# One hybrid block in fp32 on one core: two token streams interleaved by weight tiles, a lasting weight pool, and a recut gate table

## The chip, the core and the metric

The kernel runs on one core of a Trainium2 chip. TensorE (PE) multiplies, VectorE (DVE), ScalarE (ACT) and GpSimd (POOL) do element-wise work, SyncE (SP) issues DMAs; each has its own in-order instruction stream, and they meet at semaphores. Operands lie in SBUF, results of matmuls in eight PSUM banks. The metric is the device time of one launch in microseconds (us), a median over runs.

## The reference

512 tokens of width 2048, in float32, go through one block of three layers, each followed by a residual and a layer norm (`x = layer_norm(2^0.25 * x + h)`):

```
# 1: mixer
ml_q, ml_k, ml_v, ml_o, ml_i, ml_f, fx_q, fx_k, fx_v, fx_f, g_ml, g_fx = split(x @ w_in)
ml_q, ml_k = silu(causal_conv4(ml_q, ml_k))
h = norm(mlstm(ml_q, ml_k, ml_v, ml_i, ml_f)) * sigmoid(ml_o)      # 4 heads, 256 / 512 wide
y = forgetting_attention(fx_q, fx_k, fx_v, fx_f)                   # 16 heads of 128
h = (sigmoid(g_ml) * (h @ w_br_ml) + sigmoid(g_fx) * (y @ w_br_fox)) @ w_out
# 2: attention to a memory of 256 rows, 4 heads of 512
h = softmax((x @ w_xq) @ k.T) @ v @ w_xo          # k, v = split(mem @ w_xkv)
# 3: product-key experts: 8 heads, each 16 of 128*128 experts
i, g = top16 of (x @ peer_wq) against two sets of 128 keys per head
h = sum over the 128 chosen of  gelu(x . expert_u[i]) * g * expert_v[i]
```

The kernel makes each large product of three matmuls in fp32r, which carries fewer bits than fp32: an operand is split into `hi` (rounded) and `lo` (the rest), and `hi*hi + hi*lo + lo*hi` is summed in PSUM.

## The kernel before

**Streams.** The 512 tokens make two paths (class `Path`, L303): A is the first block of 128 tokens, B the other 384. A runs ahead, since B's mLSTM and attention read A's keys and values from DRAM scratch. The last layer treats tokens in two ways: for A's 128 and for the last 96 tokens the chosen experts' rows are gathered (`gathered`, L842, by indirect DMA on POOL's queue: 256 and 192 row sets of 128 x 8 KB); for the 288 between (`NDENSE`) all experts are computed densely, with a table of gates that is zero where an expert isn't chosen.

**Weight tiles.** A weight matrix comes in groups of 512 columns, a group as eight tiles of 128 x 1024 floats (512 KB). `load_w` (L160) takes one: SP loads it into a `raw` slot (`load_raw`, L125), ACT casts it to `whi` (L120), DVE subtracts to `wlo` (L123), every eighth POOL instead (L122, `SHARE`). A weight pool sets how many slots of each there are: `w1` has 5 raw, 3 hi and 2 lo and ends with the first block and the heads; `w2` 5, 3, 3 up to the end of B's attention; `w3` 3, 2, 2 after that; and `V` 3, 3, 3 for `expert_v` in the main loop. `group_ws` (L188) holds the weights still and streams 384 or 256 tokens (24 matmuls a tile), `group_as` (L203) holds the tokens still and streams the weights: 6 matmuls a tile for A, 18 for B. Matmuls of both are at L185 (`products`). PSUM has five banks `mm` for groups, and `s1`, `s2` for small products.

**Order.** Each stage is a generator that yields after a whole group. `run` (L915) drives one and, after yields whose numbers are listed by hand, lets another do its next group:

```
run(mlstm(A, ...), memory(mp), [3 * h + i for h in range(ML_H) for i in (1, 2)])
run(chain(branch_ml(A, HA, aq), fox(A, a3, at, hold_y)), heads, (5, 13, 24))
run(merge(A, YA, GA, ac, at), heads, (4,))
run(tail_a(), heads, (4, 7, 9, 13, 14))
```

So A's mLSTM takes turns with the memory's projections (L333), then A's other stages with `heads`, the mLSTM of B (L1002). `mids` (L144) is a list of small steps (softmax, transposes), of which `ride` does one after each weight tile. The framework's scheduler then orders each engine's stream by its own model, within the dependencies.

**In order of time** (us in the profile): x is loaded and split, and the gates' projections and cumulative sums made (to about 45, L236 to L287); A's mLSTM and the memory's projections (to 440); A's branches, attention (`fox`, L497), merge, `w_out` (`residual`, L633), norm (L657), cross-attention (L689), top-k, woven with the heads (to 1500); B's branches and attention (to 2410), during which the jobs of A's gathered rows go on; then the 16 tiles of y are loaded (`ytd`, L1064 to L1069: load into a work tile, split into a pair), and B's merge, `w_out`, norms and cross-attention follow (to 3100).

**The dense experts.** After B's `peer_wq`, top-k runs on DVE while `stage_a` (L1174) already multiplies: for one chunk of 128 experts two tiles of `uT`, 48 matmuls of 288 tokens, gelu, and where the result must wait, a store to DRAM (`gad`, L1188, from ACT's queue). `LOOK` = 64 chunks come before the main loop. Among them the gate table is built (L1132 to L1160): for six parts of 48 tokens, DVE makes one-hot rows (L1146, L1152), PE multiplies them (L1154), ACT copies them to four `stage` tiles (L1157), and four DMAs on ACT's queue store them (L1159):

```
gd = dp.tile([P, NC_ // 2, NDENSE // GB, 2, GB], ...)
nc.scalar.dma_start(gd[:, ch * 16:ch * 16 + 16, hb], stage[ch].rearrange("p (c q) t -> p c q t", q=2))
```

that is, in each partition 16 pieces of 2 x 48 floats. In the main loop, for each eight chunks and each quarter of the output, `stage_o` (L1214) multiplies `expert_v` tiles (24 matmuls each) by `hp`, which `stage_h` (L1192) makes from the gelu and the gate table (loaded for two chunks at a time, L1195, one piece of 2304 B a partition). Sums are added on DVE into `acc` (L1243). `fill` (L1269) puts in the remaining `stage_a` chunks and the gathered jobs of the last 96 tokens, 194 jobs: 20 (`EARLY`) before the loop, the others spread up to chunk 124. `fin` (L898) ends with the last norm and the stores.

## Time and profile before

| | |
|---|---|
| time, median of 3 runs | 5120.34 us (5119.35 to 5123.38) |
| the profiled execution | 5116.37 us, of which the span from the first to the last instruction is 5114.7 us |
| instructions in it | 74819 |
| DMA | 1421.00 MB, 278 GB/s in the mean |
| mean granted clock of PE | 0.98 |

The page of the profile has the busy time of each engine, its course in 40 slices, the DMA queues, the chain of work that ended last, and the costliest groups of instructions. Other views, which the prediction uses, are read so: "windows" gives for a stretch its length, then for each engine the busy us and the number of instructions, then PE's granted clock, the share of the DMA engines that was busy, and GB/s. "Waits" has rows `who <- whom: us in total, times, longest`. "Timeline" has start, duration, engine, line and operation, in brackets the idle time before it and what ended it. A row of "source" has the least, median and largest duration in ns. A group's row ends with busy us and mean ns of one, then idle time before it. A matmul's end is modelled, so the step from one start to the next, not the duration, is its pace.

### The profile page before, as it was taken

To read this page: it belongs to the slowest core of one execution; us is meant where nothing else is said; L and a number is where in the kernel's file an instruction comes from. 1 tells how busy PE (TensorE), PEld (TensorE's weight loads), DVE (VectorE), ACT (ScalarE), POOL (GpSimd) and SP (SyncE) were. 2 spreads that over 40 slices of the span, in tenths; PEclk is the share of its full clock that TensorE was granted. 3 is DMA by queue.
4 is the path that set the end of the run, shared out by engine and by line. 5 is a ranking of instruction groups with operands and counts; after the bars stand their busy time and mean duration, and the time that the engine had idled before them with its cause. 6 is when DMAs were issued, how large, how long until landed. Compare 5 with 4: busy or idle time off the path is not lost. (4 is left out here: it accounts for less than half of the span.)

```text
span 5114.7 us, 74819 instructions
## 1 busy us (share of the span) xinstructions
PE 4801.1 (94%) x28401; PEld 4370.3 (85%) x28401; DVE 3708.1 (72%) x5387; ACT 2114.1 (41%) x3043; POOL 1312.4 (26%) x1039
## 2 busy tenths in 40 slices
PE   7999999999999999998999999999899999999886
PEld 6877777777779999987988879998899999999875
DVE  6666676656788677776876566897667878788786
ACT  5656675455533233332324333344334333434322
POOL 1112223121233444422532312320011212122222
PEclk9999999999999999999999999999999999999998
DMA  6777897666679899876976755566689989898994
GB/s 228 270 268 260 282 312 254 221 228 206 199 280 367 335 337 345 310 266 256 348 295 235 254 204 192 201 221 203 195 309 346 347 316 359 314 356 330 341 346 178
DMA packets 405626, 1421.00 MB, mean 278 GB/s; under 512 B 93004, under 2 KB 129484, under 8 KB 346224
## 3 DMA queue, kind: packets, MB, share of 16 engines
q1 hardware_dynamic: 248032, 827.14, 46.3%
q0 software_dynamic: 89408, 551.06, 28.4%
q10 hardware_dynamic: 67824, 38.02, 2.5%
q8 instruction: 222, 3.64, 0.3%
q14 instruction: 140, 1.15, 0.1%
HBM read 1343.32 MB, written 72.62 MB: 277 GB/s over the span
## 5 line engine op out<-in xcount | busy, mean ns | idle before, releaser
L120 ACT CAST whi<-raw 128x1024 fp32r<-128x1024 f32 x1472 | 1531.6, 1051 | 2137.2 <-PE mm L185 1027.1
L123 DVE TENSOR_TENSOR wlo<-raw,whi 128x1024 fp32r<-128x1024 f32 x1352 | 1687.3, 1261 | 813.3 <-ACT whi L120 398.3
L864 DVE SCALAR_TENSOR_TENSOR xacc<-rows,dots,xacc 128x2048 f32<-128x2048 f32 x224 | 534.2, 2385 | 212.7 <-DMA rows<-in_peer_v,eid 211.7
L837 POOL DMA_INDIRECT rows<-in_peer_v,eid x224 | 356.2, 1590 | 984.0 <-DVE wlo L123 307.4
L837 POOL DMA_INDIRECT rows<-in_peer_u,eid x224 | 327.1, 1460 | 1095.4 <-DVE rows L851 443.1
L185 PE MATMUL pa<-Ch,whi 128*128 128x288 f32 x2048 | 565.0, 300 | 42.3 <-ACT whi L120 40.9
L185 PE MATMUL po<-hph,whi 128*128 128x288 f32 x2048 | 552.3, 298 | 28.6 <-ACT whi L120 14.9
L185 PE MATMUL pa<-Cl,whi 128*128 128x288 f32 x2048 | 561.7, 298 | 0.0
L185 PE MATMUL po<-hpl,whi 128*128 128x288 f32 x2048 | 549.8, 297 | 0.0
L851 DVE SCALAR_TENSOR_TENSOR rows<-rows,xacc 128x2048 f32<-128x2048 f32 x224 | 518.0, 2321 | 43.6 <-DMA rows<-in_peer_u,eid 43.2
L122 POOL TENSOR_TENSOR wlo<-raw,whi 128x1024 fp32r<-128x1024 f32 x120 | 306.5, 2554 | 849.0 <-PE mm L185 428.3
L185 PE MATMUL mm<-xh,whi 128*128 128x384 f32 x1280 | 436.1, 343 | 10.2 <-ACT whi L120 4.2
L185 PE MATMUL mm<-whi,xh 128*128 128x512 f32 x1088 | 431.4, 397 | 11.6 <-ACT whi L120 10.8
L185 PE MATMUL mm<-xl,whi 128*128 128x384 f32 x1280 | 430.1, 337 | 0.0
L185 PEld LDWEIGHTS pa<-Ch,whi 128*128 128x128 f32 x2048 | 390.3, 191 | 46.4 <-ACT whi L120 43.5
L185 PE MATMUL mm<-whi,xl 128*128 128x512 f32 x1088 | 425.7, 391 | 0.0
L185 PEld LDWEIGHTS po<-hph,whi 128*128 128x128 f32 x2048 | 383.9, 190 | 36.9 <-ACT whi L120 17.7
L185 PEld LDWEIGHTS pa<-Cl,whi 128*128 128x128 f32 x2048 | 390.5, 191 | 0.0
L185 PEld LDWEIGHTS po<-hpl,whi 128*128 128x128 f32 x2048 | 384.6, 190 | 0.8 <-issue 0.8
L185 PE MATMUL po<-hph,wlo 128*128 128x288 f32 x2048 | 335.8, 298 | 19.9 <-DVE wlo L123 19.9
L185 PE MATMUL mm<-wlo,xh 128*128 128x512 f32 x1088 | 320.3, 403 | 15.4 <-DVE wlo L123 11.8
L185 PE MATMUL pa<-Ch,wlo 128*128 128x288 f32 x2048 | 326.9, 296 | 4.5 <-DVE wlo L123 4.5
(425 smaller groups left out, 8441.8 us busy)
## 6 DMA issues: line engine op xcount, KB each, us to landing
raw<-in_w_in SPq DMA_DIRECT2D x512, 512.0 KB
raw<-in_vq SPq DMA_DIRECT2D x256, 512.0 KB
raw<-in_uT SPq DMA_DIRECT2D x256, 512.0 KB
raw<-in_w_xkv SPq DMA_DIRECT2D x64, 512.0 KB
raw<-in_w_br_ml SPq DMA_DIRECT2D x64, 512.0 KB
raw<-in_w_br_fx SPq DMA_DIRECT2D x64, 512.0 KB
raw<-in_w_out SPq DMA_DIRECT2D x64, 512.0 KB
raw<-in_w_xq SPq DMA_DIRECT2D x64, 512.0 KB
```

The lines of the kernel that those rows point to most:

```text
L120: nc.scalar.copy(hi, src)
L122: return nc.gpsimd.tensor_sub(lo, src, hi.bitcast(F32))
L123: return nc.vector.tensor_sub(lo, src, hi.bitcast(F32))
L185: nc.tensor.matmul(o, w if stat else x, x if stat else w, start=k == first and x is xh and not part, stop=k == last and part == 1)
L837: i = nc.gpsimd.indirect_dma_start(out=rows, out_offset=None, in_=I[table], in_offset=bass.IndirectOffsetOnAxis(ap=ei[:, k:k + 1], axis=0))
L851: nc.vector.scalar_tensor_tensor(rows, rows, 1.0, xacc, op0=ALU.mult, op1=ALU.mult, accum_out=dots[:, k:k + 1])
L864: nc.vector.scalar_tensor_tensor(xacc, rows, dots[:, k:k + 1], xacc, op0=ALU.mult, op1=ALU.add)
```

## The change

First, all groups yield after each weight tile, and a new `weave` drives two generators by a rate:

```diff
                 products(todo, 0, 15)
                 ride()
+                if kt < 7:
+                    yield
             for t in range(nt):
                 evac(t, banks[t])
+            yield 1 if nt == 1 else None
...
+        def weave(gen, other, rate):
+            due = 0.0
+            for extra in gen:
+                due += rate if extra is None else extra
+                while due >= 1:
+                    due -= 1
+                    next(other, None)
...
+                first = mlstm(A, a1, dict(ka=1, pre=2, qk=6, v=2, o=2, nM=1, pt=2), hold_h)
+                for _ in range(8):
+                    next(first)
...
+                gts.close()
+                with tc.tile_pool(name="mem", bufs=1, reuse_waits="tile") as mp:
+                    mem = memory(mp)
+                    weave(first, mem, 52 / 77)
+                    run(mem)
...
+                weave(chain(branch_ml(A, HA, aq), fox(A, a3, at, hold_y)), heads, 0.045)
+                weave(iter([2]), heads, 0)
                 settle()
+            weave(chain(merge(A, YA, GA, ac, at), tail_a()), heads, 0.045)
```

In place of the "..." after the eight `next` stand the transposes of the gates, which came ahead of the first group. So A's tile brings 0.045 tiles of the heads, the end of an A group a whole one, and four and two more stand ahead of and behind each norm in `tail_a` (`yield 4`, `yield 2`). A's groups and norms take their PSUM bank from a pool of their own, `ma`, with one bank, until B is alone (then five `mm` again); the two numbers are those of `mm` and `ma`:

```diff
+        banks(bk, "ps1", 4, 1)
...
-            banks = [mm_bank() for _ in range(nt)]
+            banks = [mm_bank() if nt > 1 else ma_bank() for _ in range(nt)]
```

Second, one weight pool `W` lasts for the whole kernel, and a list of rings is gone through in turn, one ring a load. The three numbers are the raw, hi and lo slots; `xs` closes after B's attention, `E` is opened ahead of the top-k, both serve from the first `stage_a` on, and `V` is gone:

```diff
+        W = weights(ctx, "w", 3, 2, 2)
+        rings[:] = [W, weights(xs, "w1", 2, 1, 1), W]
...
+        def load_raw(src, n=1024):
+            rings.append(rings.pop(0))
+            ring = rings[-1]
...
         xs.close()
+        rings[:] = [W]
-        weights(ctx, "w3", 3, 2, 2)
...
+        E = weights(ctx, "w2", 3, 3, 3)
...
+        rings[:] = [W, E]
```

Third, h and y are loaded straight into the lo tile of their pair, and y lazily, five ahead of its use in the merge, over the memory that x held (the x pools now free tile by tile):

```diff
+        def load_split(hi, lo, src):
+            nc.sync.dma_start(lo.bitcast(F32), src)
+            nc.scalar.copy(hi, lo.bitcast(F32))
+            nc.vector.tensor_sub(lo, lo.bitcast(F32), hi.bitcast(F32))
...
-            YB = []
-            for j in range(16):
-                y = tmp()
-                nc.sync.dma_start(y, ytd[j])
-                YB.append(pair(apool, "A", [P, B.n], 32))
-                split(*YB[j], y)
+                    while len(self) < min(16, j + 5):
+                        self.append(pair(apool, "A", [P, B.n], 32))
+                        load_split(*list.__getitem__(self, -1), ytd[len(self) - 1])
```

Fourth, the gate table is stored in pieces of 32 x 48 floats and loaded for four chunks at a time, and the dense stage's numbers move:

```diff
-        gd = dp.tile([P, NC_ // 2, NDENSE // GB, 2, GB], F32, tag="gd", name="gd")
+        gd = dp.tile([P, NDENSE // GB, NC_, GB], F32, tag="gd", name="gd")
...
-                nc.scalar.dma_start(gd[:, ch * 16:ch * 16 + 16, hb],
-                                    stage[ch].rearrange("p (c q) t -> p c q t", q=2))
+                nc.scalar.dma_start(gd[:, hb, ch * 32:ch * 32 + 32], stage[ch])
...
-        LOOK = 64
-        EARLY = 20
+        LOOK = 68
+        EARLY = 44
...
-            if c % 2 == 0:
-                gt = mn.tile([P, NDENSE // GB, 2, GB], F32, tag="G", bufs=2, name=nm("G"))
-                nc.sync.dma_start(gt, gd[:, c // 2])
+            if c % 4 == 0:
+                gt = mn.tile([P, NDENSE // GB, 4, GB], F32, tag="G", bufs=2, name=nm("G"))
+                nc.sync.dma_start(gt, gd[:, :, c:c + 4])
...
-            a, b = pair(mn, "hp", [P, NDENSE], 2 * J + 4)
+            a, b = pair(mn, "hp", [P, NDENSE], 2 * J + 2)
...
-                    while turn_g[0] < njobs - EARLY and turn_g[0] * (NC_ - 4) <= c * (njobs - EARLY):
+                    while turn_g[0] < njobs - EARLY and turn_g[0] * (NC_ - 16) <= c * (njobs - EARLY):
```

The last line spreads the gathered jobs up to chunk 112 instead of 124. Some work tiles have other numbers of slots (`aq` 11 for 10, `at` 5 for 6, `ht` 1 for 2, `rst` 1 for 2).

255 lines of the change are left out of this document (126 added, 129 removed).

## The prediction

> **What bounds the kernel now.** First the page: which engine is nearly always busy.
>
> ```profile
> PE 4801.1 (94%) x28401; PEld 4370.3 (85%) x28401; DVE 3708.1 (72%) x5387; ACT 2114.1 (41%) x3043; POOL 1312.4 (26%) x1039
> ```
>
> TensorE (PE) is the bound; the change takes no matmul away (both programs hold the same number), so it can only win PE's stops: 5114.7 - 4801.1 = 314 us of visible idle, and what the modelled matmul ends hide. Second, busy time by stretch; columns are PE, weight load, DVE, ACT, POOL, then granted clock, DMA share and GB/s.
>
> ```profile
> 0.00:70.00 70.00, 39.42 (x220) 31.36 (x221) 51.24 (x107) 43.87 (x77) 13.92 (x25) 0.83 0.66 223
> 70.00:440.00 370.00, 356.38 (x1865) 293.72 (x1864) 242.12 (x343) 222.42 (x269) 74.42 (x62) 1.00 0.80 268
> 440.00:1500.00 1060.00, 1006.78 (x4552) 793.10 (x4551) 717.18 (x1210) 578.40 (x791) 251.67 (x231) 0.99 0.71 244
> 1500.00:1560.00 60.00, 51.62 (x288) 50.55 (x287) 50.96 (x68) 20.28 (x29) 23.80 (x18) 0.94 0.93 351
> 2410.00:2440.00 30.00, 14.53 (x69) 13.26 (x70) 15.66 (x20) 10.54 (x19) 7.90 (x12) 0.77 0.93 336
> 3100.00:3480.00 380.00, 369.29 (x2597) 365.89 (x2596) 310.68 (x868) 149.95 (x212) 92.73 (x66) 1.00 0.58 194
> 3480.00:3750.00 270.00, 226.89 (x1664) 222.33 (x1663) 181.33 (x386) 104.53 (x328) 7.82 (x7) 0.92 0.70 208
> 3750.00:4780.00 1030.00, 1024.80 (x7713) 1020.20 (x7712) 808.33 (x896) 399.47 (x507) 219.15 (x143) 1.00 0.90 337
> 4780.00:5115.00 335.00, 249.37 (x1705) 234.57 (x1703) 263.13 (x325) 91.66 (x112) 74.96 (x49) 0.91 0.75 281
> ```
>
> Idle PE, stretch less busy: start 30.6; first block's mLSTM beside the memory projections 13.6; first block beside the heads 53.2; second weight pool 8.4; Y loaded 15.5; top-k 10.7; gate table 43.1; main loop 5.2; tail 85.6. The clock adds to it: 0.92 over 270 us is, at a half speed, 2 x 0.08 x 270 = 43 us throttled, 22 us lost. The sum below is made against the profiled execution, 5116.37 us (span 5114.7 and 1.7 around it), 4.0 us under the median of 5120.34.
>
> **Part by part. 1. Weaving by weight tiles.** Two paces of PE, from starts of matmuls that follow each other:
>
> ```profile
> 504.45 0.39 PE L185 MATMUL mm<-whi,Ch 128*128 128x512 f32 x1
> 504.69 0.39 PE L185 MATMUL mm<-whi,Cl 128*128 128x512 f32 x1
> ```
>
> ```profile
> 467.23 0.33 PE L185 MATMUL mm<-xh,whi 128*128 128x384 f32 x1
> ...
> 470.00 1.55 PE L185 MATMUL mm<-xh,wlo 128*128 128x384 f32 x8
> 471.38 0.33 PE L185 MATMUL mm<-xh,whi 128*128 128x384 f32 x1
> ```
>
> A tile of the first block is six matmuls, 6 x 0.235 = 1.41 us; one of the other stream is 471.38 - 467.23 = 4.15 us. Each is 524,288 bytes, so a run of the first block's tiles asks 372 GB/s; no stretch above moves more than 351. What a run does reach, in the queue's timeline:
>
> ```profile
> 500.74 19.10 SPq L128 DMA_DIRECT2D raw<-in_w_br_ml  x11
> ```
>
> and who waits from 440 to 1480 us (total, times, longest):
>
> ```profile
> SPq L128 <- DVE wlo L123: 560.3, 279, 11.1
> ACT whi L120 <- DMA raw<-in_w_in: 47.2, 73, 3.4
> PE mm L185 <- DVE wlo L123: 23.1, 40, 1.9
> PE mm L185 <- ACT whi L120: 13.2, 20, 2.1
> ```
>
> Eleven issues in 19.10 us are ten steps of 1.88 us. The queue waits for raw slots, casts wait for landings, PE for the split: supply is short in such runs, while an 8-tile group of the other stream (33 us) leaves the queue idle with its five slots full. Woven, eight first-block tiles bring 7 x 0.045 + 1 = 1.3 tiles of the heads: 8 x 1.41 + 1.3 x 4.15 = 16.7 us for 9.3 tiles, 292 GB/s, under what the rows show. The gain lies between the visible 53 us and 40 groups x 8 x (1.88 - 1.41) = 150; nothing is the lower end if DVE's bursts, not supply, make the stops. I take **75**: half the upper end, since norms and softmax chains keep theirs. For the stretch before, 13.6 us idle, I take 8 of 0 to 14. The Trainium skill, page "DMA: Bandwidth & Descriptors", section Specifications, puts a core's HBM limit at about 358 GB/s. By it the run of 372 must stop and the woven 292 need not, which would give 95 here and 4910 us in all; the 351 of 1500 to 1560 agrees with such a ceiling.
>
> The price: first-block groups now share one PSUM bank ("ma"), so the next group's first matmul waits for the copy that empties it.
>
> ```profile
> L120 ACT CAST whi<-raw 128x1024 fp32r<-128x1024 f32 x1472 | 1531.6, 1051 | 2137.2 <-PE mm L185 1027.1
> ```
>
> ```profile
> L320 ACT COPY at<-mm x36: 573/586/599, 39.1 to 1371.6; 128x512 f32<-128x512 f32 x36
> ```
>
> The copy is 0.59 us, with a cast of 1.05 ahead of it on ACT at most 1.64; 56 groups, 0 to 92 us. In the new instruction order a tile of the other stream, up to 4.15 us, stands between most groups and covers it: **-10**. The tiles' splits are the same instructions; lo has three slots where it had two, hi three and raw five as before.
>
> **2. Start.** The gate transposes stand behind ten tiles instead of eight, but ahead of the first memory tile, so PE still waits for the gate chain: two tiles' 2.8 us, I take 3 of the 30.6.
>
> **3. One lasting pool.** At 1500 to 1560 the second pool no longer waits for the first one's buffers: 5 of the idle 8.4, bounds 0 and 8. In top-k (idle 10.7) uT tiles have six raw and five hi and lo slots instead of three and two; DVE, 310.68 of 380 busy, is the other limit: 5, bounds 0 and 11.
>
> **4. Y over x.** At 2410 one wait stands out:
>
> ```profile
> PE mm L185 <- ACT Ah L120: 15.2, 1, 15.2
> ```
>
> Sixteen loads and splits stood between attention and merge; now each row lands in its lo tile, five ahead, and the merge's matmuls follow the attention's directly. The first row must still wait for x's last reader and for DMA, cast and split. 15.2 idle and half of the throttled 2 x 0.23 x 30 = 14 make 22; I take **15**, bounds 5 and 22.
>
> **5. Gate table in large pieces.** Issue times in ns (least, median, most) of its stores on ACT's queue, of ACT's store of 128 pieces of 1152 B (gad) and of SP's load of 128 pieces of 4096 B (uT); then ACT's timeline around three gate stores; then that stretch's waits:
>
> ```profile
> L1159 ACTq DMA_DIRECT2D gd<-stage x24: 377/2607/6355, 3489.4 to 3730.4; - x24
> ...
> L1188 ACTq DMA_DIRECT2D gad<-ga x126: 326/327/2018, 3243.9 to 4777.8; - x126
> ```
>
> ```profile
> L128 SPq DMA_DIRECT2D raw<-in_uT x256: 327/328/877, 3204.5 to 4754.2; - x128
> ```
>
> ```profile
> 3625.95 11.55 ACTq L1159 DMA_DIRECT2D gd<-stage x3
> 3637.61 1.99 ACT L120 CAST whi<-raw 128x1024 fp32r<-128x1024 f32 x2 [11.60 <-issue]
> ```
>
> ```profile
> ACT whi L120 <- issue: 56.2, 7, 12.3
> PE pa L185 <- ACT whi L120: 34.2, 7, 8.4
> ```
>
> Three issues hold ACT for 11.55 us, casts stand behind them, and PE stands for the casts: 34.2 us, and 22 us of clock, 56 together. The new store has 128 pieces of 6144 B instead of 2048 of 384 B; by the gad and uT rows, alike over a factor of 3.6 in bytes, 24 issues cost 8 us instead of 24 x 2.6 = 63. DVE is late next: the new order has 19 gathered rows beside these matmuls where this stretch had 8,
>
> ```profile
> L851 DVE SCALAR_TENSOR_TENSOR rows<-rows,xacc 128x2048 f32<-128x2048 f32 x8 | 18.3, 2292 | 10.8 <-DMA rows<-in_peer_u,eid 10.8
> ```
>
> so 181 + 11 x 2.3 = 207 of about 215 us. Hence **40**, not 56; bounds 15 and 56. The Trainium skill, same page, section "Issuing engines are not separate DMA queues", says that the sequencer's time to initiate a DMA is usually small beside the DMA. By it this term would be nearly nothing and the time 4970, as in rival C. The rows differ: 11.55 us of issue for three stores, with the casts behind it. The loads of G go the other way, 768 pieces instead of 128, 32 instead of 64 of them: on SP, whose waits are for slots, and in a loop where PE idles 5 us in 1030: I take 2 lost with the two "hp" slots fewer, bounds 0 and 10.
>
> **6. Gathers done earlier.** From 4780 on a wait, the pace of the main loop's matmuls, and PE's last stretch on the chain:
>
> ```profile
> DVE xacc L864 <- DMA rows<-in_peer_v,eid: 23.9, 12, 6.9
> ```
>
> ```profile
> 3799.88 0.29 PE L185 MATMUL po<-hph,whi 128*128 128x288 f32 x1
> 3800.01 0.30 PE L185 MATMUL po<-hpl,whi 128*128 128x288 f32 x1
> ```
>
> ```profile
> 5075.30 1.26 PE po L1249 x10
> ```
>
> DVE stands for gathered rows, with splits and PSUM adds queued behind. The stretch's 1705 matmuls at 0.132 us are 225 us; with the 38 us from 5076.6 to the end 263, against 335: 72 us lost. In the new order the last gathered row stands 35 DVE splits of 3.2 us ahead of the end (before: two), and rows come singly, not in threes; 44 of the 194 jobs move to the quieter stretch before. The 38 us of output stay: **50**, bounds 20 and 72.
>
> Sum: 75 + 8 - 10 + 3 + 5 + 5 + 15 + 40 - 2 + 50 = 189. 5116.4 - 189 = 4927, and with 4 to the median **4930**.
>
> **Rivals.** *A: weaving yields nothing*, because DVE's bursts (conversions, softmax, one tensor after another) and not supply stop PE: DVE is 717 of 1060 busy there, and PE's two rows name the split more than the cast. Then 75 and 8 go, 106 is left: 5116 - 106 + 4 = 5014. *B: slower, by POOL's splits.* Every eighth tile is split on POOL:
>
> ```profile
> L122 POOL TENSOR_TENSOR wlo<-raw,whi 128x1024 fp32r<-128x1024 f32 x120 | 306.5, 2554 | 849.0 <-PE mm L185 428.3
> ```
>
> Before, that tile was always the last of its group, and another stream's loads often came next; woven, it falls anywhere, and with one lo slot in the small pool and a fixed rotation all loads behind it stand. The 64 memory, 448 first-block and 72 heads' tiles up to 1500 us hold 584 / 8 = 73 of them; if each shows its 2.55 us, 186 are lost against 189 - 83 = 106 won elsewhere: 5116 + 80 + 4 = 5200. It decides from 106 / 73 = 1.5 us a tile. Against it: a heads' tile of 4.15 us is longer than POOL's split. *C: the gate term is nothing*, because a store of 768 KB holds ACT however it is cut, or DVE takes PE's place as what is late: 40 goes, 4970; the uT row, 0.33 us for 512 KB, speaks against the first. *D: the change doesn't do what it says*, the scheduler undoing the weave: the new instruction order shows 24 matmuls of the heads inside nearly every first-block group, so I leave it out.
>
> **Chances.** Forecast, 4860 to 4985 with C in it: 0.62. A, 4985 to 5060: 0.20. B and other losses of its size: 0.10, of which a tenth lands near no change. Better than 4860, where weaving, tail and gate reach their upper ends (94 more in all): 0.08. The range **4860 to 5040** holds 0.8. About 0.2% (10 us) is what a measurement here can tell from no change: faster 0.88, same 0.03, slower 0.09.
>
> **What would show it.** Right: the queue's loads of first-block tiles evenly 1.8 us apart and PE idle of 440 to 1500 halved; the gate stores under 0.5 us each and no cast waiting for issue; no wait for "Ah"; no gathered row in the last 100 us, PE busy to its last matmul. Wrong: PE waiting for POOL's split or for the "ma" copy (B), PE idle before 1500 unchanged (A), or the main loop no longer at 1024.8 of 1030 because the woven slots or the shorter "hp" ring starve it.

## The result, and the profile after

| | before | after |
|---|---|---|
| median of 4 runs | 5121.86 us (5119.35 to 5124.33) | 5068.13 us (5062.06 to 5072.05) |
| the profiled execution | 5116.37 us, span 5114.7 | 5072.05 us, span 5070.3 |
| after / before | | 0.9894, 95% interval 0.9877 to 0.9911 |

The changed kernel is 54 us faster. 4930 was forecast, so 138 us of the forecast gain are missing. The page of the changed kernel, busy time of each engine:

```profile
PE 4789.3 (94%) x28401; PEld 4397.2 (87%) x28401; DVE 3728.7 (74%) x5387; ACT 2122.9 (42%) x3046; POOL 1270.4 (25%) x1039
```

Visible idle time of PE is 5070.3 - 4789.3 = 281 us instead of 314. Its stretches, cut where the stages end in this kernel (length, busy time of PE, weight load, DVE, ACT, POOL, granted clock, DMA share, GB/s):

```profile
0.00:70.00 70.00, 41.47 (x209) 32.30 (x210) 54.09 (x109) 42.04 (x76) 12.92 (x25) 0.80 0.69 233
70.00:430.00 360.00, 349.04 (x1884) 297.79 (x1883) 247.08 (x332) 216.96 (x265) 75.45 (x58) 1.00 0.81 269
430.00:1425.00 995.00, 961.47 (x4456) 784.87 (x4456) 724.91 (x1203) 573.28 (x790) 251.21 (x236) 0.99 0.77 261
1425.00:1555.00 130.00, 112.88 (x590) 105.03 (x589) 92.84 (x127) 41.01 (x59) 43.52 (x31) 0.92 0.83 306
2385.00:2460.00 75.00, 54.41 (x232) 48.77 (x231) 38.06 (x39) 18.46 (x33) 22.13 (x25) 0.85 0.69 240
3460.00:3740.00 280.00, 266.57 (x2025) 263.71 (x2024) 233.58 (x429) 123.57 (x329) 26.09 (x22) 0.98 0.75 272
3740.00:3800.00 60.00, 39.69 (x269) 37.08 (x268) 37.23 (x96) 20.46 (x74) 1.70 (x2) 0.86 0.60 216
3800.00:4900.00 1100.00, 1080.01 (x8017) 1069.23 (x8016) 892.32 (x981) 430.26 (x529) 232.54 (x157) 0.99 0.92 343
4900.00:5040.00 140.00, 127.72 (x908) 121.99 (x909) 78.99 (x117) 44.89 (x54) 4.50 (x5) 0.95 0.45 149
```

The first block's stretch idles 33 us in 995, where it was 53 in 1060; the gate table's stretch 13 in 280, where it was 43 in 270; the last stretch 12 in 140, where it was 86 in 335 (38 of these the output). But 1425 to 1555, the merge at 2385 and the first 60 us of the main loop have new holes, and the main loop stops for 20 us in 1100, where it was 5 in 1030.

**A ledger.** The stages lie at other times in the two kernels, so they are compared at equal work: for every start of a matmul, the usual step (from one start to the next, of matmuls of its shape, 30th percentile in the trace of before) is summed; a run is "ahead" by the time that it reaches the same sum earlier. One run is good to some 5 us either way, so two can differ by 10 for no cause: seven kernels whose code is the changed kernel's up to the end of the first block are 38.8 to 48.6 ahead there. What one stage wins or loses is steadier. Columns: the time at which the kernel before has done that much work, and its stage; last, the difference of the spans. All in us, positive is ahead of the kernel before.

| run | 434 memory | 1474 first block | 2001 B's branches | 2562 y, merge | 3447 top-k | 3698 gate table | 3814 loop starts | 4725 loop | span |
|---|---|---|---|---|---|---|---|---|---|
| after | 9.5 | 48.6 | 42.0 | 9.4 | 2.5 | 28.8 | 16.1 | -14.2 | 44.4 |
| weave8 | -28.2 | -98.7 | -102.0 | -125.6 | -120.6 | -97.0 | -112.1 | -151.6 | -89.6 |
| weave8_mm5 | -0.3 | -43.7 | -51.3 | -62.4 | -60.1 | -36.5 | -49.5 | -84.7 | -21.7 |
| listed | -8.1 | -34.4 | -64.9 | -105.1 | -111.3 | -79.5 | -107.2 | -150.0 | -89.5 |
| before_rings | -3.0 | -31.3 | -49.8 | -57.9 | -64.4 | -61.0 | -60.8 | -63.5 | -55.2 |
| one_ring | 12.2 | 67.9 | 61.6 | 18.7 | 17.7 | 40.4 | 26.5 | -9.9 | 50.6 |
| one_ring_eager | 15.9 | 72.3 | 66.5 | 41.2 | 38.9 | 57.1 | 35.5 | -0.8 | 55.7 |
| eager_y | 9.8 | 41.7 | 35.2 | 16.7 | 14.3 | 41.6 | 28.2 | -5.5 | 56.6 |
| before_gate | 0.7 | -3.1 | -5.9 | -5.5 | -6.9 | 38.2 | 53.1 | 41.8 | 2.6 |
| before_half | -2.1 | -3.1 | -6.2 | -4.8 | -12.2 | -8.2 | -7.6 | -25.9 | 22.8 |
| before_gate_half | -2.3 | -2.3 | -5.4 | -3.6 | -11.5 | 35.8 | 49.5 | 11.2 | 60.3 |
| after_half | 9.1 | 44.7 | 38.2 | 13.4 | 20.7 | 52.6 | 22.0 | -27.8 | 36.9 |
| apart | 8.9 | 41.4 | 34.1 | 2.8 | -2.3 | 23.3 | 37.2 | 14.3 | 24.4 |
| apart_fast | 9.0 | 45.2 | 37.0 | 10.8 | 9.0 | 36.0 | 50.3 | -60.2 | 14.8 |
| late | 6.6 | 38.8 | 32.2 | 3.9 | 2.8 | 41.2 | 30.9 | 3.1 | 37.7 |
| before_turn | 0.3 | -0.3 | -3.8 | -4.5 | -11.1 | -9.6 | -17.7 | -32.0 | 12.1 |
| before_early | 0.2 | 4.6 | 1.8 | 4.6 | -23.6 | -38.4 | -47.9 | -52.3 | -7.3 |
| hybrid_eager | 9.5 | 48.0 | 42.4 | 25.3 | 19.1 | 44.9 | 59.4 | -8.4 | 52.7 |
| best_mid | 14.4 | 71.0 | 65.7 | 47.6 | 45.4 | 69.9 | 54.1 | 23.3 | 79.2 |

The row of the changed kernel says where to look: 49 us won up to the end of the first block, nearly all of them lost again by 3447, 26 won by the gate table and 43 lost in the main loop, 59 won in the last stretch.

### The profile page after: what moved, and what is told of

Its sections match the earlier page's. It is cut to its first block, busy times and chain, and to the rows that moved or that the text cites. A ratio compares the mean times of both kernels' runs of the same rounds, so it can differ in the third digit from the quotient of the medians.

```text
span 5070.3 us, 74427 instructions
## 1 busy us (share of the span) xinstructions
PE 4789.3 (94%) x28401; PEld 4397.2 (87%) x28401; DVE 3728.7 (74%) x5387; ACT 2122.9 (42%) x3046; POOL 1270.4 (25%) x1039
## 5 line engine op out<-in xcount | busy, mean ns | idle before, releaser
L846 POOL DMA_INDIRECT rows<-in_peer_v,eid x224 | 336.0, 1500 | 1010.8 <-DVE wlo L137 389.5
L205 PE MATMUL pa<-Ch,whi 128*128 128x288 f32 x2048 | 564.8, 300 | 14.4 <-ACT ga L1223 13.0
L846 POOL DMA_INDIRECT rows<-in_peer_u,eid x224 | 309.6, 1382 | 1037.1 <-DVE rows L860 320.4
L205 PE MATMUL po<-hph,whi 128*128 128x288 f32 x2048 | 533.6, 298 | 32.6 <-ACT hph L134 27.3
L205 PE MATMUL po<-hpl,whi 128*128 128x288 f32 x2048 | 533.1, 297 | 6.1 <-DVE hpl L137 6.1
L205 PEld LDWEIGHTS pa<-Ch,whi 128*128 128x128 f32 x2048 | 389.8, 190 | 18.3 <-ACT ga L1223 14.8
L205 PE MATMUL po<-hph,wlo 128*128 128x288 f32 x2048 | 349.5, 298 | 6.0 <-DVE wlo L137 6.0
L205 PEld LDWEIGHTS po<-hph,wlo 128*128 128x128 f32 x2048 | 301.5, 191 | 6.5 <-DVE wlo L137 6.5
L205 PEld LDWEIGHTS pa<-Ch,wlo 128*128 128x128 f32 x2048 | 289.8, 189 | 4.7 <-DVE wlo L137 3.9
L205 PE MATMUL mm<-xh,wlo 128*128 128x384 f32 x1280 | 258.5, 337 | 5.3 <-DVE wlo L137 5.3
```

The costliest lines, as they stand in the source:

```text
L205: nc.tensor.matmul(o, w if stat else x, x if stat else w, start=k == first and x is xh and not part, stop=k == last and part == 1)
L846: i = nc.gpsimd.indirect_dma_start(out=rows, out_offset=None, in_=I[table], in_offset=bass.IndirectOffsetOnAxis(ap=ei[:, k:k + 1], axis=0))
```

## The experiments

Each time below is a median; the ratio is to the kernel before on the same chip, with its 95% interval. The runs lie on several chips, so differences of a few us go by the ratios. The changed kernel's is 0.9894, 5068 us.

### The first block: tiles, banks, rings

**weave8.** The other stream driven in whole groups, at the rates of the change.

```diff
-                while due >= 1:
-                    due -= 1
-                    next(other, None)
+                while due >= 8:
+                    due -= 8
+                    for _ in range(8):
+                        next(other, None)
```

> Base is the changed kernel, 5068 us. The same rates, but the other stream is driven eight tiles (a whole group) at a time instead of single tiles; banks and rings as changed. Theory S (the supply of weight tiles is short in runs of the first block, and mixing by tiles evens it out; 50 us were won up to the end of the first block at equal work): 30 to 50 us more, 5098 to 5118. Rival A of the prediction (DVE's bursts stop PE, and what was won there came from elsewhere, such as the sixth lo slot or the bank of its own): 5068 within 6.

5204.59 us, 1.0163 (1.0145 to 1.0182): 136 us more than the changed kernel, far above the 30 to 50 expected. Who waits in it from 440 to 1480 us:

```profile
PE ma L205 <- ACT at L340: 43.4, 25, 3.8
PE ma L205 <- DVE ra L655: 14.3, 4, 5.3
```

Runs of the first block's groups stand for the copy that empties their one bank. So the price of the one bank is hidden only as long as tiles of the other stream stand between the groups, as they do in the changed kernel; another arrangement was needed to weigh the mixing itself.

**weave8_mm5.** The same, with the first block's groups in the five common banks again.

```diff
-        banks(bk, "ps1", 4, 1)
+        banks(bk, "ps1", 5, 0)
```

> Base is the changed kernel (5068 us) with the other stream driven by groups of eight tiles, which gave 5205; here the first block's groups take their banks from the five common ones again instead of the single bank of their own. Theory S (mixing by tiles wins 40 to 50 of supply; the rest of the 136 us was the single bank, each of whose copies a run of the first block's groups must wait for): 5105 to 5125, as the kernel before in that stretch. Rival (all of the 136 was the bank; mixing by tiles wins nothing, the gain up to 1500 us came from the rings): 5068 within 8.

5146.00 us, 1.0061 (1.0040 to 1.0083). The bank was 52 (by the ratios) to 58 of the 136, and some 80 remain; but that is slower than the kernel before too. Both theories missed: something else in the changed kernel costs time where the order is by groups.

**listed.** Five common banks, and groups of the other stream at the places that the kernel before lists by hand.

```diff
+                if n in groups and extra == 1 or extra == 2 and ("norm", twos) in groups:
+                    for _ in range(8):
+                        next(other, None)
...
-            weave(chain(merge(A, YA, GA, ac, at), tail_a()), heads, 0.045)
+            weave(chain(merge(A, YA, GA, ac, at), tail_a()), heads, (4, 8, 10, 12, 16, ("norm", 2)))
```

> Base is the changed kernel (5068 us). The other stream is driven in whole groups at the places listed in the kernel before, and banks are the five common ones; rings and all else as changed. Groups at an even rate gave 5146. Theory S (mixing by tiles wins 40 to 50 against the listed order, which had itself won some 35 against an even rate by standing where norms and softmax leave PE idle): 5108 to 5120. Rival (the listed places are worth nothing; by groups it is 5146 either way): 5138 to 5150. Rival (the rings in turn had brought the gain): 5068 within 8.

5204.06 us, 1.0159 (1.0134 to 1.0185): none of the three. Up to 1474 us of the kernel before it has the same order of groups as that kernel and the same banks, and is 34 us behind it in the ledger. What differs there are the rings in turn and the trimmed work tiles (and small things: h's loads, the start). Its waits of PE from 440 to 1500 us are mostly for cast and split:

```profile
PE mm L205 <- ACT whi L134: 27.9, 35, 2.3
PE mm L205 <- DVE wlo L137: 24.3, 29, 2.0
```

**before_rings.** The rings and the trimmed tiles alone, put into the kernel before.

```diff
-        weights(x0, "w1", 5, 3, 2)
+        weights(x0, "w1", 3, 2, 2)
+        two = [dict(W)]
+        weights(x0, "w1b", 2, 1, 1)
+        two.append(dict(W))
+        turns[:] = [two[0], two[1], two[0]]
...
+            if turns:
+                turns.append(turns.pop(0))
+            ring = turns[-1] if turns else ring or W
```

(with s 5 for 6, ht 1 for 2, rst 1 for 2 slots)

> The kernel before (5120 us) with its first weight pool (5, 3, 2, up to the end of the heads) cut into two rings in turn (3, 2, 2 and 2, 1, 1), and the work tiles trimmed as in the change to make room (s 5 for 6, ht 1 for 2, rst 1 for 2); order, banks and all else as before. Theory R2: 30 to 65 more up to 1600 us, 5150 to 5185. Rival L (the rings cost nothing): 5120 within 6.

5167.92 us, 1.0091 (1.0061 to 1.0122): 49 us more, as theory R2 said; 31 of them up to the end of the first block and 18 up to 2001, these nearly all between 1500 and 1550, where the second pool takes over. Its waits from 440 to 1480 us, of PE and of ACT:

```profile
PE mm L193 <- ACT whi L125: 35.5, 41, 2.9
PE mm L193 <- DVE wlo L128: 24.5, 28, 2.0
```

```profile
ACT whi L125 <- DMA raw<-in_w_in: 78.7, 64, 4.3
```

In the kernel before these were 13.2, 23.1 and 47.2 (rows in the prediction): a cast waits longer for its tile to land, and PE for the cast. Where a cast can be matched to its load by the semaphore it waits for (four fifths of them, 440 to 1400 us), 70 of 324 casts are of a tile loaded earlier than that of the cast before; in the kernel before none of 343. In both nearly all five raw slots (4.96 and 4.97 in the mean) are in use. So the number of slots and their filling are alike, and the tile that is needed next is often the later load.

**one_ring.** The changed kernel with one ring of 5, 3 and 3 slots up to the end of B's attention.

```diff
-        W = weights(ctx, "w", 3, 2, 2)
...
-        rings[:] = [W, weights(xs, "w1", 2, 1, 1), W]
+        rings[:] = [weights(xs, "w1", 5, 3, 3)]
...
         xs.close()
+        W = weights(ctx, "w", 3, 2, 2)
         rings[:] = [W]
```

> Base is the changed kernel (5068 us). Up to the end of B's attention all weight tiles take one ring of 5 raw, 3 hi and 3 lo slots instead of two rings (3, 2, 2 and 2, 1, 1) in turn, and the lasting pool is opened after that; the weave by tiles, banks, y, the gate table and the dense stage as changed. Theory R2 (the two rings cost some 30 us or more up to 1560 us, which the mixing by tiles wins and more, and some 10 in B's attention): 25 to 45 less, 5023 to 5043. Rival L (the slots are the same in number, so nothing: the group-wise runs of 5146 and 5204 were slow for other reasons, such as trimmed work tiles): 5068 within 6.

5058.04 us, 0.9880 (0.9844 to 0.9916): 7 less by the ratios, and the intervals overlap: neither of the two expected times. In its place the gain is there: 67.9 ahead instead of 48.6 at the end of the first block, and no cast of 327 out of the order of the loads (85 of 316 in the changed kernel). By the end 6 of the 19 are left; see below for where such gains go.

### y ahead of the merge

**eager_y.** y loaded as in the kernel before.

```diff
-            class Rows(list):
...
-            YB = Rows()
+            YB = []
+            for j in range(16):
+                y = tmp()
+                nc.sync.dma_start(y, ytd[j])
+                YB.append(pair(apool, "A", [P, B.n], 32))
+                split(*YB[j], y)
```

> Base is the changed kernel, 5068 us. Here y is loaded as in the kernel before: all 16 rows into a work tile, each split into its pair, ahead of the merge; all else is as changed. At equal matmul work the changed kernel loses 21 us against the kernel before between the last steps of B's attention and the first merge group. Theory Y (rows that come five ahead reach their pair too late, a dozen short stops of PE, each with a drop of the clock): 15 to 25 us less, 5043 to 5053. Rival (the loss belongs to DVE's gathered rows, which fall on other steps now, and not to y): 5068 within 5. The prediction's own step (lazy rows win 15) would give 5083.

5065.43 us, 0.9900 (0.9883 to 0.9917): the same time as the changed kernel. In its place (2323 to 2562 us of before) it loses 4.6 where the changed kernel loses 21.0. That is more than chance: of the runs with the changed kernel's code up to there, the five with lazy y lose 15 to 22, the two with y ahead (this and hybrid_eager) 3 to 5. (weave8 and weave8_mm5, whose order differs, lose 11 and 9 with lazy y.) The profiled execution was 7 us behind that of the changed kernel already at the end of the first block, whose code is the same, and is 12 ahead at the end; but the medians lie 3 apart, so the time alone would not have shown the 16 us.

**one_ring_eager.** Both edits.

> The run with one ring up to the end of B's attention and, besides, y loaded ahead of the merge as in the kernel before. If both theories hold: 8 to 15 less than with one ring alone, 5010 to 5035. If rings and y are worth nothing: 5068 within 6.

5049.34 us, 0.9856 (0.9828 to 0.9884), 12 less than with one ring alone by the ratios, with intervals that overlap; the difference was expected so, the time wasn't. In its place it loses 10.8 where one_ring loses 29.4.

### The gate table

**before_gate.** The kernel before with the fourth part alone (store, load for four chunks, hp two slots shorter), lines as in the change's diff.

> The kernel before (5120 us) with the fourth part alone: the gate table stored in 128 pieces of 6144 B, loaded for four chunks at a time, hp's ring two shorter; no other change. The prediction's step: 40 less for the stores, 2 more for the loads: 5082. By the ledger at equal work of the changed kernel: 23 to 26 less for the stores and up to 13 more where the loop starts: 5095 to 5110. Rival C (a store holds ACT however it is cut): 5120 within 5.

5109.48 us, 0.9978 (0.9967 to 0.9989): 11 less, much less than 40. But in its place the step won more than forecast, 45 us from 3447 to 3698 and 15 more up to 3814. Its stretches there, in the loop and in the last part:

```profile
3480.00:3750.00 270.00, 268.63 (x2110) 268.05 (x2109) 202.93 (x408) 128.83 (x358) 8.49 (x9) 1.00 0.69 249
3750.00:4600.00 850.00, 849.42 (x6418) 849.18 (x6417) 668.37 (x720) 330.62 (x422) 145.47 (x109) 1.00 0.91 337
4600.00:5074.00 474.00, 398.26 (x2615) 373.18 (x2613) 362.70 (x435) 139.15 (x169) 95.41 (x76) 0.92 0.81 300
```

PE runs without a hole until 4600, and from there idles 76 us and runs at 0.92. The gain is given back at the end, where PE now has 64 sets of gathered rows left behind uT's last tile (see the table under apart).

### The dense stage: what sets its end

**before_half** and **before_gate_half.** Every second set of gathered rows of the last 96 tokens isn't loaded, in the kernel before and in before_gate; the set in SBUF is used again, so the sums are other numbers. The same edit stands at `peer_u`.

```diff
-                rows = gather_rows("peer_v", ei, k, last)
+                if i == 0 or k % 2 == 0:
+                    rows = gather_rows("peer_v", ei, k, last)
```

> The kernel before (5120 us); of the gathered rows of the last 96 tokens every second set isn't loaded (the row set in SBUF is used again, so those two sums are other numbers): about 96 MB less traffic, the same work on DVE and PE. Theory M (from 3800 us on memory traffic at about 350 GB/s sets the end: 419 MB were left there, 1197 us, beside 1193 us of matmuls): the last stretch's loss goes, 50 to 70 less, 5050 to 5070. Rival D (DVE's sums over gathered rows set it): 5110 to 5120.

> The kernel before with the gate table recut and every second set of gathered rows not loaded as in the run beside it. With all rows the recut table was 53 us ahead at 3800 us and 11 at the end. Theory M (given back to memory traffic): with half the rows the gain is kept, 45 to 55 less than the run with half the rows alone, 4995 to 5025. Rival D (given back to DVE, whose work is the same): 10 less than that run, or 5100 to 5110.

5081.98 us, 0.9918 (0.9893 to 0.9943), and 5042.79, 0.9846 (0.9823 to 0.9870). Half of the rows' loads left out win 38 us, less than expected; and then the recut table is worth 39 us instead of 11, nearer to theory M's 45 to 55 than to rival D's 10. But the edit did more than it says: PE's order is fixed when the kernel is built, and with fewer loads the scheduler spread uT's tiles to the end (before_half; in the kernel before its last matmul starts at 4775.8):

```profile
L185 PE MATMUL pa<-Ch,whi x2048: 289/295/608, 3232.2 to 4966.6; 128*128 128x288 f32 x187
```

So neither traffic nor DVE is shown by these two runs. Why the order matters, the next run tells.

**apart.** The changed kernel with a ring each for uT and expert_v in the main loop.

```diff
+                rings[:] = [E]
                 vh, vl, _ = load_pair(I["vq"][c0 // 2 + m, q])
+                rings[:] = [W]
```

> Base is the changed kernel, 5068 us. In the main loop expert_v's tiles use only the second ring (3, 3, 3) and uT's only the lasting one (3, 2, 2), as in the kernel before; until the loop both serve in turn as changed. At equal work the main loop loses 30 us against the kernel before. Theory R (going through the rings in turn ties the two kinds of tiles together, so that a cast or split waits for a slot that the other kind holds): 15 to 30 us less, 5038 to 5053. Rival P (it comes of the gathered rows, which are spread over 112 chunks instead of 124 and begin earlier, or of the shorter ring of hp): 5068 within 5.

5089.88 us, 0.9941 (0.9924 to 0.9957): 24 us more, against both theories, and still R is half right. By 4624 us of the kernel before it has gained 50 us on the changed kernel, and from there to 4976 it loses 73. Its waits from 4640 to 4960 us:

```profile
ACT whi L134 <- DMA raw<-in_vq: 104.8, 32, 7.1
```

The first and the last of uT's matmuls, from before, from the changed kernel, from apart and from before_gate:

```profile
L185 PE MATMUL pa<-Ch,whi x2048: 289/295/608, 3222.7 to 4775.8; 128*128 128x288 f32 x187
```

```profile
L205 PE MATMUL pa<-Ch,whi x2048: 289/295/609, 3210.9 to 4971.5; 128*128 128x288 f32 x187
```

```profile
L205 PE MATMUL pa<-Ch,whi x2048: 289/295/588, 3215.7 to 4614.9; 128*128 128x288 f32 x187
```

```profile
L185 PE MATMUL pa<-Ch,whi x2048: 289/295/442, 3228.6 to 4643.8; 128*128 128x288 f32 x187
```

With a ring of its own uT runs ahead and is used up at 4776, 4615 and 4644 us, and in all three the bad stretch begins there. With the rings in turn uT lasts to 4972. What is bad is not expert_v by itself: in apart_fast (below), when uT and the rows are both used up, PE runs on expert_v alone without a hole:

```profile
4780.00:4900.00 120.00, 119.99 (x901) 119.42 (x901) 73.35 (x110) 45.91 (x54) 0.00 (x0) 1.00 0.63 211
```

It is expert_v together with gathered rows. Of the 192 row sets of the last 96 tokens, so many are summed on DVE after uT's last matmul (of all its operand pairs, where the rows above show one), and so long PE stands idle between that matmul and the last set:

| run | uT's last matmul at (us) | sets after it | idle PE (us) |
|---|---|---|---|
| before | 4777 | 43 | 47.5 |
| before_gate | 4648 | 64 | 75.3 |
| apart | 4616 | 52 | 46.2 |
| apart_fast | 4495 | 52 | 66.3 |
| before_early | 4829 | 25 | 19.0 |
| before_half | 4968 | 6 | 9.5 |
| before_turn | 4978 | 9 | 11.2 |
| late | 4946 | 8 | 14.8 |
| after | 4973 | 0 | 0 |

That is 0.8 to 1.9 us a set. Whether PE waits there for the rows' loads or for DVE's sums, no run parts.

**before_turn.** Rings in turn in the dense stage alone, in the kernel before.

```diff
+            if both:
+                both.append(both.pop(0))
+            ring = both[-1] if both else ring or W
...
+        V = dict(pool=gap, raw=3, hi=3, lo=3)
+        both[:] = [W, V]
```

> The kernel before (5120 us) with one thing alone: from the dense experts on, the tiles of uT and of expert_v take the two weight rings (3, 2, 2 and 3, 3, 3) in turn, instead of one ring each; gathered jobs, gate table and all else as before. Theory T (rings in turn keep the two kinds of tiles in step, so that uT isn't used up 200 us early and the last stretch isn't of expert_v alone, where DVE is short; it costs at the loop's start and in the loop): 15 to 40 less, 5080 to 5105, with the last stretch 50 to 60 shorter and the loop longer. Rival (the prediction's step 6: the tail is short since the gathered rows are done earlier; rings in turn only cost): 5125 to 5150.

5098.16 us, 0.9964 (0.9950 to 0.9979): 18 less, as theory T said: 21 lost from 3447 to 4725, 44 won after it, where uT now lasts to 4978.

**late** and **before_early.** The gathered jobs as before, in the changed kernel; and as changed, in the kernel before (step 6 alone).

```diff
-        LOOK = 68
-        EARLY = 44
+        LOOK = 64
+        EARLY = 20
...
-                    while turn_g[0] < njobs - EARLY and turn_g[0] * (NC_ - 16) <= c * (njobs - EARLY):
+                    while turn_g[0] < njobs - EARLY and turn_g[0] * (NC_ - 4) <= c * (njobs - EARLY):
```

> Base is the changed kernel, 5068 us. The gathered jobs as in the kernel before: LOOK 64, EARLY 20, spread up to chunk 124; all else as changed. The prediction's step (the early gathers win 50 in the tail, and nothing is lost elsewhere): 5118. Theory P (they win 58 in the tail but cost about 13 where the main loop starts, since DVE ends the gate table later, and 10 to 20 in the loop): 5093 to 5107. Rival (the tail's gain comes of something else): 5068 within 5.

> The kernel before (5120 us) with LOOK 68, EARLY 44 and the gathered jobs spread up to chunk 112: step 6 of the prediction alone. By that step: 50 less, 5070. Theory M (memory traffic sets the end; 24 row sets of 1 MB, moved ahead of the main loop at 350 GB/s, are up to 69 us, less what the gate stage can't take beside its own work): 20 to 50 less, 5070 to 5100. Rival (from the run with the gathers as before, which lost nothing against the changed kernel): 5120 within 6.

late: 5065.64 us, 0.9892 (0.9875 to 0.9909), no difference from the changed kernel. before_early: 5128.76, 1.0029 (1.0012 to 1.0046), 10 to 15 us slower: 48 lost by 3814, in top-k and the gate table, where DVE has the rows beside its own work, and 45 won back after 4725. In sum step 6 is worth nothing or less.

**apart_fast.** apart, with the jobs spread only up to chunk 80 (`NC_ - 48`).

> Base is the run with the rings apart (5090 us): at equal work it was 50 us ahead of the changed kernel at chunk 110 or so and lost 73 in the last 300 us, in which only expert_v's tiles are left. Here the gathered jobs are also spread only up to chunk 80 instead of 112. Theory D (once uT is used up each expert_v tile of 3.2 us of PE brings DVE about 2.1 us of splits and sums and two thirds of a gathered row at 2.35 us, 3.7 together, so that DVE sets the pace; without the rows it doesn't): 40 to 70 us less, 5020 to 5050. Rival (three slots are too few for tiles of expert_v alone, whatever DVE does): 5090 within 10.

5103.34 us, 0.9970 (0.9957 to 0.9983): 13 us more than apart, and neither expected time. Theory D's number missed, but its case did not come about: in the new order uT is used up earlier too (4495), 52 sets still stand behind it, and the hole is at 4500 to 4780. The rival's three slots are enough, by the row of 4780 to 4900 above.

**hybrid_eager.** y as before; rings apart up to chunk 40, in turn from there.

```diff
+                apart = c0 < 40
+                if apart:
+                    rings[:] = [E]
                 vh, vl, _ = load_pair(I["vq"][c0 // 2 + m, q])
+                if apart:
+                    rings[:] = [W]
+                elif len(rings) < 2:
+                    rings[:] = [W, E]
```

> Base is the changed kernel (5068 us). y is loaded ahead of the merge as in the kernel before; in the main loop the rings are apart up to chunk 40, so that uT's tiles fill PE while the first gate table load waits for the last store, and in turn from there, so that uT lasts to the end. If the parts add up (27 at the loop's start, 10 to 15 for y): 5025 to 5035. Rival M (what is won at the loop's start is given back to memory traffic later): 5053 to 5063.

5060.38 us, 0.9868 (0.9836 to 0.9899), the time of rival M, but not its cause: the loop's start is won (59.4 ahead at 3814), and 41 us are lost again by 4220, where the order changes over.

**after_half.** Half of the rows' loads left out as above, in the changed kernel.

> The changed kernel (5068 us), every second set of gathered rows of the last 96 tokens not loaded (the set in SBUF is used again, so those two sums are other numbers): about 96 MB less traffic, the same work on DVE and PE. Between 3300 and 4300 us of matmul work the changed kernel lost 43 us against the kernel before. Theory M (that loss is memory traffic's): 30 to 45 less, 5023 to 5038. Rival R (it is the order of the tiles in two rings taken in turn, with the wait for the first gate load): 5055 to 5068.

5074.12 us, 0.9917 (0.9886 to 0.9949): no gain at all. Its main loop, beside the changed kernel's row above:

```profile
3800.00:4900.00 1100.00, 1060.52 (x7827) 1050.38 (x7826) 879.81 (x966) 417.12 (x517) 112.14 (x80) 0.99 0.75 268
```

With 268 GB/s instead of 343 PE is busy no more than before. So theory M fell for the changed kernel: in its order, where uT lasts to the end, the loads of rows are no bound. Its short stops in the loop belong to the rings in turn, since apart, which changes nothing else, hasn't got them up to 4624; what in the rings makes them was not tested.

### A better version

**best_mid.** one_ring_eager with LOOK 66, EARLY 32 and the jobs up to chunk 120.

> One ring up to the end of B's attention and y ahead of the merge (5049 us, base of this run), with the gathered jobs set midway between the two kernels: LOOK 66, EARLY 32, spread up to chunk 120. In that base memory traffic was at nine tenths up to about 4900 us and at a tenth in the last 50. Theory M (the rows moved to the quiet end relieve the loop): 5 to 15 less, 5034 to 5044. Rival (what is won in the loop is lost in the last stretch, as with the gathers wholly as before): 5049 within 6.

5037.19 us (5030.03 to 5040.60), 0.9840 (0.9817 to 0.9863): faster than both kernels, by some 28 us than the changed one by the ratios. The 8 it has over its base lie within overlapping intervals, and their cause is not settled; after_half speaks against theory M's traffic.

## Why the prediction was wrong, step by step

5068 lies above the range, between the times of rivals A and B and by the mechanism of neither. What failed: step 3 and the term of the main loop, which counted slots and not the order in which two rings are filled and used; step 4, where the rows of y come too late one by one; and step 6, which left out what its early rows cost.

| step, and its stretch in the kernel before | forecast | in the changed kernel |
|---|---|---|
| start, memory (to 434) | 11 | 9.5 |
| weave and "ma" bank (to 1474) | 65 | 39.1 |
| lasting pool (to 2001) | 5 | -6.6 |
| B's attention (to 2323) | 0 | -11.6 |
| y over x (to 2562) | 15 | -21.0 |
| the rest of B (to 3233) | 0 | 2.3 |
| top-k (to 3447) | 5 | -9.2 |
| gate table (to 3698) | 40 | 26.3 |
| main loop, with its start (to 4725) | -2 | -43.0 |
| gathers earlier, tail | 50 | 58.6 |
| sum | 189 | 44.4 |

**Step 1, the weave, was right, in size too.** 76 were forecast up to the end of the first block. With one ring the weave is 68 to 72 ahead (one_ring, one_ring_eager, best_mid); with two rings it is worth 73 to 83 (38.8 to 48.6, against -34.4 of listed). (The one ring has one lo slot more than the kernel before; no run weighs that alone.) That cast and split came too late was the cause: in the changed kernel SP's loads in a run of the first block

```profile
442.25 33.18 SPq L148 DMA_DIRECT2D raw<-in_w_in  x19
```

are 33.18 / 18 = 1.84 us apart through tiles of both streams, and PE hardly waits from 430 to 1425 us:

```profile
PE sm L345 <- ACT at L340: 6.4, 4, 2.1
PE ma L205 <- POOL wlo L136: 4.9, 6, 1.4
PE ma L205 <- DVE wlo L137: 4.2, 7, 1.9
PE mm L205 <- ACT whi L134: 3.5, 5, 1.7
PE ma L205 <- DVE ra L655: 2.9, 1, 2.9
...
PE ma L205 <- ACT at L540: 1.4, 2, 1.0
```

With the same rings and whole groups (listed) 27.9 and 24.3 stand for cast and split. So rival A fell, and rival B too (4.9 us of POOL's splits, not 186). The "ma" bank costs 4.3 us of waits (2.9 for ra, 1.4 for at) where its step put 10, as long as tiles stand between the groups; without them it is 52 to 58. The sign that the step named came only in part: the loads are as even as it said, but PE's visible idle time fell from 53 to 33 us and was not halved.

The sentence beside it on the ceiling was of no use. The Trainium skill, page "DMA: Bandwidth & Descriptors", section Specifications, has 358 GB/s for a core; its section "Measured (HBM→SBUF, 128 partitions, SWDGE, issued from GpSimd)" says that this is the share when the pair's other core streams as well, and has 425 for one core alone. The kernel before goes past the former:

```profile
1480.00:1600.00 120.00, 106.65 (x570) 100.20 (x569) 102.01 (x131) 40.02 (x57) 44.31 (x33) 0.96 0.96 374
```

374 GB/s for 120 us, more than the 351 on which the rule had been leaned, and more than the run of 372 asks.

**Step 3 failed**, and with it the line under step 1 that the splits "are the same instructions; lo has three slots where it had two, hi three and raw five as before". Slots were counted, and not the order in which they are filled. Two rings in turn cost 31 us with groups (before_rings) and 19 to 33 with tiles (68 to 72 ahead with one ring, 39 to 49 with two), in step 1's stretch; the step had them at nothing there. (one_ring keeps the trimmed work tiles, so these aren't the cause.) That it is the loads out of order is what the traces suggest; a run with two rings and the loads in order was not made.

**Step 4 failed.** "The merge's matmuls follow the attention's directly": they did, one by one. The one wait of 15.2 us became ten short ones, of 17.8 us together, with the clock at 0.85 over 75 us:

```profile
DVE xacc L873 <- DMA rows<-in_peer_v,eid: 22.4, 7, 6.7
...
ACT Ah L141 <- DMA Al<-ytd: 12.4, 5, 5.1
PE mm L205 <- DVE Al L142: 11.6, 6, 3.6
...
PE mm L205 <- ACT Ah L141: 6.2, 4, 2.9
```

(waits of the changed kernel, 2385 to 2460 us). From PE's timeline, the stops in two weight tiles:

```profile
2404.76 0.96 PE L205 MATMUL mm<-Ah,whi 128*128 128x384 f32 x4
2409.36 1.59 PE L205 MATMUL mm<-Al,whi 128*128 128x384 f32 x4 [3.63 <-DVE Al L142]
...
2414.82 0.96 PE L205 MATMUL mm<-Ah,whi 128*128 128x384 f32 x4 [0.16 <-ACT Ah L141]
2416.51 0.98 PE L205 MATMUL mm<-Al,whi 128*128 128x384 f32 x4 [0.72 <-DVE Al L142]
2420.43 1.65 PE L205 MATMUL mm<-Ah,whi 128*128 128x384 f32 x4 [2.94 <-ACT Ah L141]
```

A tile with its two rows takes 2414.82 - 2404.76 = 10 us instead of 4.15: rows of y wait for their own landing (12.4 us) and for a DVE that stands 22.4 us for gathered rows, and PE goes at their pace. Loaded ahead, they cost 3 to 11 us (eager_y, hybrid_eager, one_ring_eager, best_mid) instead of 15 to 29.

**Step 5 was right in kind and its gain did not last.** The store's issue in the changed kernel (least, median, most, in ns):

```profile
L1195 ACTq DMA_DIRECT2D gd<-stage x24: 326/861/1832, 3541.9 to 3770.6; - x24
```

is a third of the 2607, not an eighth: 24 x 0.86 = 21 us, where 8 were forecast. The 34.2 us that PE stood for casts there are gone. Alone the step won 45 in its place (before_gate), and 26 in the changed kernel, since with the gathers early DVE is late there, as the step said; late wins 38. What the step left out is the end: in before_gate's order uT is used up early, 64 row sets stand behind it, and of PE's gain 11 us are left.

**The main loop failed the most, -43 for -2.** The step spoke of G's pieces and "hp" slots, and had nothing on the rings taken in turn. At the start SP has three tiles of expert_v in flight, and then the load of G, which waits for the last store (issued at 3770.6):

```profile
3739.33 8.48 SPq L148 DMA_DIRECT2D raw<-in_vq  x3
3777.57 0.62 SPq L1232 DMA_DIRECT2D G<-gd  x1
```

```profile
PE po L205 <- ACT hph L134: 14.4, 1, 14.4
```

PE stands for 14.4 us, and the clock drops. With the rings apart uT's tiles fill the hole (13.9 won instead of 12.7 lost). The 30 us after it are short stops; apart hasn't got them up to 4624, and they are not the rows' traffic (after_half).

**Step 6 had the right number by half of its cause, and left out the price.** 50 forecast, 58.6 found. What it read is there: late rows hold PE, 43 sets of them in the kernel before. But two parts of the change take sets away from behind uT's last tile. The early gathers alone (before_early) leave 25 and win 45 in the last stretch; they lose 48 by 3814, of which step 5 had allowed for 16 and no step for the rest. The rings in turn alone (before_turn) keep uT to the end, leave 9 sets and win 44 there, the very thing that costs in the loop; their net is 18 to 24 us won. In the changed kernel, without the early gathers (late), 34.6 of the 58.6 remain, and about as much as is lost there, 23, is won between 2562 and 4725, so that the time is the same.

**Not settled:** the 7 us lost between 1474 and 2001 (all of it up to 1550, at the hand-over to B) and the 12 in B's attention, which one_ring and eager_y lose as well, so that neither rings nor y explain them; and the 9 us in top-k.

## What to carry to other kernels

Two rings with as many slots together as one are not one ring: look at the order in which loads are issued against the order of use. A gain counts only if what sets the end of a later stage is moved as well, so ask for every stage what would be late if PE were early; and compare two kernels at equal work, since a total can hide a gain of 60 and a loss of 50. When a step's number comes out right, undo it alone before you believe its cause. And look at the order of the tiles after every edit: leaving out loads made the scheduler order the matmuls anew, so that a run meant to weigh traffic weighed the order too.

## What the runs showed of the hardware

Short stops of PE cost more than their length. In the traces of before, of after and of listed the granted clock drops to half 96 times between 100 and 4900 us. In each trace these drops start whole multiples of 3.413 us apart (to 4 ns). What decides is how long PE stood in the 3.413 us that end there, in one piece or in several: a drop followed in 1 of 3930 such windows with under 1.4 us of idle time, in 19 of 56 with 1.4 to 2 us, and in 76 of 76 with more (windows already at half clock are not counted). Around the stop of 3.63 us above the clock is

```profile
2408.00:2413.00 5.00, 3.64 (x12) 3.64 (x13) 2.91 (x4) 0.00 (x0) 1.34 (x2) 0.66 0.76 256
```

The Trainium skill, page "TensorE: Matmul & The Clock Gate", section "HAM oscillation — how this bites in real kernels", warns of gaps of over about 3.4 us; here 2 us in such a window were enough, so that many short waits cost clock as well as time.

The issue of a DMA on ACT's queue grows with its number of pieces, but not in proportion: 2607 ns for 2048 pieces, 861 to 906 ns (median, after and before_gate) for 128 pieces of 6144 B, and 327 ns for 128 pieces of 1152 B (row of gad in the prediction). But the least of each lie close together, 377, 326 and 326 ns, so how full the queue is may count for more than the number or the size of the pieces; no run parts these.
